# A two-block transformer kernel on one core: the expert gates of token tile 0 as split fp32r products, routing over 112 sums, and a new routing order

## The chip, the cores and the metric

The kernel runs on one core of a Trainium2 chip. The metric is the device time of one execution in microseconds (us). TensorE multiplies matrices, VectorE and ScalarE work elementwise, GpSimd (POOL) issues the gather and scatter transfers, SyncE issues the large loads. Each engine runs its own instructions in the order in which they are written and waits where a tile that it needs isn't ready, or a buffer isn't free.

## The reference

Two transformer blocks on 256 tokens of width 1024. The change lies in the last part of the second block, a layer of 16384 experts (`peer_ffn`). For each of 256 tokens and 8 heads:

```python
q = (xn @ w_q).reshape(B, S, 8, 2, 64)
s = einsum('bshpd,hpkd->bshpk', q, sub_keys)          # two score rows of 128 a head
v_half, i_half = top_k(s, 16)                         # the 16 best of each
cand = v_half[..., 0, :, None] + v_half[..., 1, None, :]   # 16 x 16 sums
top_s, top_c = top_k(cand.reshape(..., 256), 16)      # the 16 best sums
i1 = take(i_half[..., 0, :], top_c // 16); i2 = take(i_half[..., 1, :], top_c % 16)
experts = i1 * 128 + i2;  g = softmax(top_s)
u = expert_u[experts]                                 # 128 experts a token
act = gelu(einsum('cd,ced->ce', x, u))
out = einsum('ce,ced->cd', g * act, expert_v[experts])
```

## The kernel before, in words

The kernel doesn't gather experts. It multiplies all tokens with all 16384 rows of `u`, and all weighted activations with all rows of `v`, and a table of gates [expert, token] that is zero nearly everywhere picks what counts.

**U part.** A loop of 128 steps (`for i in range(P)`). Step i multiplies one block of 128 experts (1024 x 128 of `u`) with the 256 tokens. To keep fp32 accuracy with the fast fp32r format, a number is split into a high half (rounded to fp32r) and a low half (the rest), and a product is three fp32r products: `u_mm` issues 24 TensorE matmuls of 256 columns (L1029 to L1031). `u_load` loads the block and makes its high half on ScalarE (L1016), `u_low` makes its low half on VectorE (L1021), both for step i + 2 while step i runs. `u_act` applies the gelu to step i - 1 on ScalarE; steps below 88 send the result to memory from ScalarE's queue (L1041, L1042), later ones keep it (`kept`, L1038). The high halves have three buffers.

**Routing.** VectorE fills what the products leave it. `route` yields small pieces with an estimated cost each: `half` (the 16 best of 128 scores, by MAX8, FIND_INDEX8 and MATCH_REPLACE8), `both` (256 sums and the 16 best of them), `places` and `pick` (back from positions to indices), `share` (softmax). A generator `steps` gives the order: tile 1 (tokens 128 to 255) in four pairs of heads, then tile 0 with its 8 heads together. In step i pieces are issued while the estimated VectorE time `dve` is below TensorE's `pe`.

**Gates of tile 1** go through memory: `share` computes addresses and `scatter` issues 16 indirect transfers a head on GpSimd (L1085), 128 in all; a head's wait for those of the head before. `g_load` reads the table back (L1199), and its first load waits for the last head's scatters.

**Gates of tile 0** are made on chip. `turn` transposes indices and gates (L1099) once tile 0 is routed. Then one group of 4 tokens is made in each step, 32 groups in all: `g_prep` makes two one-hot rows a token on VectorE (two instructions of 512 elements, L1178) and multiplies the second by the gate (L1180); in the next step `g_mm` multiplies the two one-hots of a token, 128 x 128 in fp32, 4 matmuls a group (L1186, each stands twice in the trace), and in the step after that ScalarE copies 4 tokens' gates into the table `gb` (L1187).

**V part.** 128 steps of 12 matmuls of 512 columns (L1293 to L1295), whose weights are activations times gates (`w_mul`, `w_split`).

From the U part on, the order on TensorE, VectorE, ScalarE and SyncE is the order in which the code is written.

Of the kernel before, what the change touches and what calls it, by code (L numbers as in the profile page):

```python
# [10 lines left out]
F32 = mybir.dt.float32  # L11
F32R = mybir.dt.float32r
U32 = mybir.dt.uint32
AF = mybir.ActivationFunctionType
# [5 lines left out]
P = 128  # L20
# [151 lines left out]
def tile_block(ctx, tc, d, out, NK=40, CONV="0.2 0.2 1.1 1.1 1.2", K1=4, M0=7, MR=65, ML=8, MQ=40, WB=3, NTAIL=2, WARM=7):  # L172
# [4 lines left out]
    def nm(s):  # L177
        uid[0] += 1
        return f"{s}_{uid[0]}"
# [813 lines left out]
    with ExitStack() as sc_:  # L993
        pc = Even(sc_.enter_context(tc.tile_pool(name="pc", bufs=1)))
        act_d = dram.tile([P - NK, P, S], F32, name="act_d")
        iT = pc.tile([P, 2, P], F32, name="iT")
        gT = pc.tile([P, P], F32, name="gT")
        gb = pc.tile([P, P, P], F32, name="gb")
        ixr = pc.tile([P, 8, 16], U32, name="ixr")
        gtr = pc.tile([P, 8, 16], F32, name="gtr")  # L1000
# [65 lines left out]
                                                            for e in ("PE", "DVE", "Activation", "SP")}))  # L1066
        i16 = cst[:, C_I16:C_I16 + 16]
        tok = cst[:, C_TOK:C_TOK + 1]
        later = []
        SYNC = mybir.DependencyInfo(mybir.DependencyClass.Sync, mybir.DependencyReason.DATA)  # L1070

        def top16(src, vv, ii, tag, w):
# [22 lines left out]
        def turn(sel):  # L1095

            t = gp()[:, 0:384].rearrange("p (i t) -> p i t", i=3)
            for i in range(3):
                T.transpose(t[:, i, :], sel[:, i].rearrange("p h s -> p (h s)"), ident)  # L1099
            A.activation(iT, t[:, 0:2], AF.Copy)  # L1100
            A.activation(gT, t[:, 2, :], AF.Copy)
            done.append(0)

        def route(tt, heads, sel):

            n = len(heads)
            H = slice(heads[0], heads[0] + n)
            vals = rk.tile([P, 8, 2, 16], F32, name=nm("vals"), tag="vals", bufs=1)
            idx = rk.tile([P, 8, 2, 16], U32, name=nm("idx"), tag="idx", bufs=1)
            tv = rk.tile([P, 8, 16], F32, name=nm("tv"), tag="tv")  # L1110
            ti = rk.tile([P, 8, 16], U32, name=nm("ti"), tag="ti", bufs=1)
            te = rk.tile([P, 8, 16], F32, name=nm("te"), tag="te")
            idf = rk.tile([P, 8, 2, 16], F32, name=nm("idf"), tag="idf", bufs=1)
            ab = rk.tile([P, 2, 8, 16], U32, name=nm("ab"), tag="ab", bufs=1)
            abf = rk.tile([P, 2, 8, 16], F32, name=nm("abf"), tag="abf", bufs=1)

            def half(k, p_):
                top16(sco[:, tt, heads[k], p_, :], vals[:, k, p_, :], idx[:, k, p_, :], "mr", P)

            def both(k):  # L1120
                cand = rk.tile([P, 16, 16], F32, name=nm("cand"), tag="cand")
                V.tensor_tensor(cand, vals[:, k, 0, :, None].to_broadcast([P, 16, 16]),
                                vals[:, k, 1, None, :].to_broadcast([P, 16, 16]), op=OP.add)
                top16(cand.rearrange("p a b -> p (a b)"), tv[:, k, :], ti[:, k, :], "mc", S)

            def places():
                V.tensor_tensor(te[:, :n], tv[:, :n], tv[:, :n, 0:1].to_broadcast([P, n, 16]), op=OP.subtract)
                V.tensor_copy(idf[:, :n], idx[:, :n])
                V.tensor_scalar(ab[:, 0, :n], ti[:, :n], 4, None, op0=OP.logical_shift_right)
                V.tensor_scalar(ab[:, 1, :n], ti[:, :n], 15, None, op0=OP.bitwise_and)  # L1130
                V.tensor_copy(abf[:, :, :n], ab[:, :, :n])
                later.append(lambda: A.activation(te[:, :n], te[:, :n], AF.Exp))

            def pick(p_, k0, m):
                k_ = slice(k0, k0 + m)
                e_ = rk.tile([P, 4, 16, 16], F32, name=nm("eq"), tag="eq")[:, :m]
                V.tensor_tensor(e_, abf[:, p_, k_, :, None].to_broadcast([P, m, 16, 16]),
                                i16[:, None, None, :].to_broadcast([P, m, 16, 16]), op=OP.is_equal)
                V.tensor_tensor(e_, e_, idf[:, k_, p_, None, :].to_broadcast([P, m, 16, 16]), op=OP.mult)
                V.tensor_reduce(sel[:, p_, heads[0] + k0:heads[0] + k0 + m, :], e_, axis=AX.X, op=OP.add)  # L1140

            def share():
                zs = rk.tile([P, 8], F32, name=nm("zs"), tag="zs")
                V.tensor_reduce(zs[:, :n], te[:, :n], axis=AX.X, op=OP.add)
                V.reciprocal(zs[:, :n], zs[:, :n])
                dst = gtr[:, H] if tt else sel[:, 2, H]
                V.tensor_tensor(dst, te[:, :n], zs[:, :n, None].to_broadcast([P, n, 16]), op=OP.mult)
                if tt == 0:
                    later.append(lambda: turn(sel))
                    return  # L1150
                f = rk.tile([P, 8, 16], F32, name=nm("cf"), tag="cf", bufs=1)
                V.scalar_tensor_tensor(f[:, :n], sel[:, 1, H], float(P), tok[:, :, None].to_broadcast([P, n, 16]),
                                       op0=OP.mult, op1=OP.add)
                V.scalar_tensor_tensor(ixr[:, H], sel[:, 0, H], float(P * P), f[:, :n], op0=OP.mult, op1=OP.add)
                for h in heads:
                    scatter(h)

            for k in range(n):
                for p_ in range(2):
                    yield 1.57, lambda k=k, p_=p_: half(k, p_)  # L1160
            for k in range(n):
                yield 2.75, lambda k=k: both(k)
            yield 1.4 if n > 4 else 1.0, places
            for p_ in range(2):
                for k0 in range(0, n, 4):
                    m = min(4, n - k0)
                    yield 0.9 * m, lambda p_=p_, k0=k0, m=m: pick(p_, k0, m)
            yield 1.2, share


        iota = cst[:, C_IOTA:C_IOTA + P]

        def g_prep(t4):

            t_ = slice(4 * t4, 4 * t4 + 4)
            oh = [po_.tile([P, 4, P], F32, name=nm("oh"), tag=f"oh{i}", bufs=2) for i in range(2)]
            for i, o in enumerate(oh):
                V.tensor_tensor(o, iota[:, None, :].to_broadcast([P, 4, P]),  # L1178
                                iT[:, i, t_, None].to_broadcast([P, 4, P]), op=OP.is_equal)
            V.tensor_tensor(oh[1], oh[1], gT[:, t_, None].to_broadcast([P, 4, P]), op=OP.mult)  # L1180
            later.append(lambda: g_mm(t4, oh))

        def g_mm(t4, oh):
            pt = ga_().rearrange("p (t i) -> p t i", t=4)
            for q_ in range(4):
                T.matmul(pt[:, q_, :], oh[0][:, q_, :], oh[1][:, q_, :], start=True, stop=True)  # L1186
            later.append(lambda: A.activation(gb[:, :, 4 * t4:4 * t4 + 4], pt.rearrange("p t i -> p i t"), AF.Copy))  # L1187


        pw = None  # L1190
# [41 lines left out]
        def w_step():  # L1232
            if not ws and wq_:
                w_mul(wq_.pop(0))
            if ws:
                k = next(iter(ws))
                if wq_:
# [5 lines left out]
        done = []  # L1243
        sel1 = pr.tile([P, 2, 8, 16], F32, name="sel1")
        sel0 = pr.tile([P, 3, 8, 16], F32, name="sel0")
        steps = (st_ for tt, heads, sel in ((1, (0, 1), sel1), (1, (2, 3), sel1), (1, (4, 5), sel1), (1, (6, 7), sel1),
                                            (0, tuple(range(8)), sel0)) for st_ in route(tt, heads, sel))
        nxt = next(steps)
        g_left = list(range(P // 4))
        dve, pe = 0.0, 0.0  # L1250
# [1 line left out]
        for i in range(P):  # L1252

            now, later = later, []
            q = p
            p = u_mm(*prep.pop(0))
            if q is not None:
                u_act(i - 1, q)
            for f in now:
                f()  # L1260
            h = u_load(i + 2)
            dve += 1.2
            pe += 2.9

            if g_left and done:
                g_prep(g_left.pop(0))
                dve += 2.0
                pe += 0.88
            while nxt is not None and dve < pe:
                dve += nxt[0]  # L1270
                nxt[1]()
                nxt = next(steps, None)
            if i >= P - 2:
                w_step()
            prep.append(u_low(*h))
            if nxt is None and pw is None and done:
                sr.close()
                pk = Even(sg_.enter_context(tc.tile_pool(name="pk", bufs=1)))
                kept.append(pk.tile([P, NK, S], F32, name="kept"))
                pw = Even(sg_.enter_context(tc.tile_pool(name="pw", bufs=1, side="right")))  # L1280
            if i == P - 12:
                for _ in range(3):
                    a_load()
                    g_load()
        u_act(P - 1, p)
        assert not g_left and not later

        pO = [[op_(), op_()], [gp(), gp()]]

# [82 lines left out]
```

## Time and profile before

| | |
|---|---|
| time, median of 3 runs | 1203.9 us (1203.32 to 1205.07) |
| the profiled execution: its time, its span | 1205.83 us, 1204.0 us |
| TensorE busy | 1165.1 us, 97% |
| VectorE busy | 929.2 us, 77% |
| ScalarE busy | 634.6 us, 53% |
| GpSimd busy | 335.4 us, 28% |
| the U part (first to last matmul of L1029) | 443.3 to 842.8 us |

Busy shares are means over stages with different limits, so the rows further down are taken by stage. [...]

### The profile page before, as it was taken

To read this page: it belongs to the slowest core of one execution; us is meant where nothing else is said; L and a number is where in the kernel's file an instruction comes from. 1 tells how busy PE (TensorE), PEld (TensorE's weight loads), DVE (VectorE), ACT (ScalarE), POOL (GpSimd) and SP (SyncE) were. 2 spreads that over 40 slices of the span, in tenths; PEclk is the share of its full clock that TensorE was granted. 3 is DMA by queue.
4 is the path that set the end of the run, shared out by engine and by line. 5 is a ranking of instruction groups with operands and counts; after the bars stand their busy time and mean duration, and the time that the engine had idled before them with its cause. 6 is when DMAs were issued, how large, how long until landed. Compare 5 with 4: busy or idle time off the path is not lost.

```text
span 1204.0 us, 20173 instructions
## 1 busy us (share of the span) xinstructions
PE 1165.1 (97%) x7282; PEld 1043.8 (87%) x7282; DVE 929.2 (77%) x1907; ACT 634.6 (53%) x1050; POOL 335.4 (28%) x278
## 2 busy tenths in 40 slices
PE   8999999979998899999999999999999999999995
PEld 7777886869997799999999999999888888888884
DVE  5786978976676849999999888854777777777775
ACT  6557554575345555555545555554545555555553
POOL 2001200022012002787778778400111111111102
PEclk9999999989899899999999999999999999999998
DMA  8876689749454557889888886645877777778773
GB/s 288 291 251 247 241 232 349 272 153 378 149 202 149 151 172 233 225 220 238 225 232 211 206 169 142 192 161 182 256 244 248 253 250 249 251 248 256 255 229 134
DMA packets 103315, 271.94 MB, mean 226 GB/s; under 512 B 28637, under 2 KB 40421, under 8 KB 102704
## 3 DMA queue, kind: packets, MB, share of 16 engines
q1 hardware_dynamic: 62352, 225.03, 57.0%
q0 software_dynamic: 27616, 31.87, 12.4%
q10 hardware_dynamic: 13248, 13.77, 3.4%
q8 instruction: 57, 0.93, 0.3%
q14 instruction: 42, 0.34, 0.1%
HBM read 248.51 MB, written 23.68 MB: 226 GB/s over the span
## 4 chain that ended last, share of the span: by engine, by line
PE 83%; DVE 6%; DMA 4%; ACT 2%; issue 2%; POOL 1%; SPq 0%; ACTq 0%; POOLq 0%; DVEq 0%
PE sc L1031 10%; PE sc L1030 10%; PE sc L1029 10%; PE po L1293 5%; PE po L1294 5%; PE po L1295 5%; PE pg L1293 5%; PE pg L1294 5%; PE pg L1295 5%; PE pg L279 4%; PE pg L280 4%; PE pg L278 4%; PE pg L1186 2%; DVE wl L253 2%; DMA wf<-in_w_in_dram 2%
## 5 line engine op out<-in xcount | busy, mean ns | idle before, releaser
L1021 DVE TENSOR_TENSOR wl<-wf,wh 128x1024 fp32r<-128x1024 f32 x256 | 311.9, 1221 | 107.2 <-ACT wh L1016 105.0
L1029 PE MATMUL sc<-hThi,wh 128*128 128x256 f32 x1024 | 292.5, 286 | 0.0
L1031 PE MATMUL sc<-hThi,wl 128*128 128x256 f32 x1024 | 290.5, 284 | 0.8 <-DVE wl L1021 0.5
L1030 PE MATMUL sc<-hTlo,wh 128*128 128x256 f32 x1024 | 289.7, 283 | 0.0
L1016 ACT ACTIVATE wh<-wf 128x1024 fp32r<-128x1024 f32 x256 | 268.9, 1050 | 38.1 <-ACT act L1041 15.3
L1085 POOL DMA_INDIRECT g_d<-gtr,ixr x128 | 231.1, 1806 | 123.8 <-ACT act L1041 64.0
L1031 PEld LDWEIGHTS sc<-hThi,wl 128*128 128x128 f32 x1024 | 196.3, 192 | 2.0 <-DVE wl L1021 1.5
L1029 PEld LDWEIGHTS sc<-hThi,wh 128*128 128x128 f32 x1024 | 196.6, 192 | 0.0
L1030 PEld LDWEIGHTS sc<-hTlo,wh 128*128 128x128 f32 x1024 | 196.4, 192 | 0.0
L253 DVE TENSOR_TENSOR wl<-wf,wh 128x1024 fp32r<-128x1024 f32 (+3 forms) x121 | 138.4, 1151 | 58.8 <-ACT wh L252 58.5
L252 ACT ACTIVATE wh<-wf 128x1024 fp32r<-128x1024 f32 (+3 forms) x121 | 120.2, 996 | 114.2 <-PE pg L280 57.2
L252 ACT ACTIVATE wwh<-w 128x256 fp32r<-128x256 f32 x128 | 53.5, 418 | 167.7 <-PE pg L1294 167.7
L278 PE MATMUL pg<-wh,hThi 128*128 128x512 f32 (+1 forms) x264 | 102.2, 388 | 1.7 <-ACT hThi L345 1.7
L279 PE MATMUL pg<-wl,hThi 128*128 128x512 f32 (+1 forms) x264 | 102.8, 389 | 0.4 <-DVE wl L253 0.4
L280 PE MATMUL pg<-wh,hTlo 128*128 128x512 f32 (+1 forms) x264 | 102.1, 388 | 0.0
L1293 PE MATMUL po<-wh,wwh 128*128 128x512 f32 x256 | 99.6, 389 | 0.0
L1294 PE MATMUL po<-wl,wwh 128*128 128x512 f32 x256 | 99.6, 389 | 0.0
L1295 PE MATMUL po<-wh,wwl 128*128 128x512 f32 x256 | 99.6, 389 | 0.0
L1293 PE MATMUL pg<-wh,wwh 128*128 128x512 f32 x256 | 99.6, 389 | 0.0
L1294 PE MATMUL pg<-wl,wwh 128*128 128x512 f32 x256 | 99.6, 389 | 0.0
L1295 PE MATMUL pg<-wh,wwl 128*128 128x512 f32 x256 | 99.6, 389 | 0.0
L1211 POOL DMA_DIRECT2D actl<-act_d x44 | 31.9, 725 | 189.0 <-DVE w L1219 108.8
(384 smaller groups left out, 2066.5 us busy)
## 6 DMA issues: line engine op xcount, KB each, us to landing
wf<-in_u_dram SPq DMA_DIRECT2D x128, 512.0 KB
wf<-in_v_dram SPq DMA_DIRECT2D x128, 512.0 KB
wf<-in_w_in_dram SPq DMA_DIRECT2D x68, 512.0 KB
wm<-in_w_mod_dram SPq DMA_DIRECT2D x48, 512.0 KB
act_d<-act ACTq DMA_DIRECT2D x88, 128.0 KB
actl<-act_d POOLq DMA_DIRECT2D x44, 256.0 KB
wf<-in_w_out_dram SPq DMA_DIRECT2D x16, 512.0 KB
g_d<-zero POOLq DMA_DIRECT2D x16, 512.0 KB
```

What stands on the lines that cost most here:

```text
L252: A.activation(hi, src, AF.Copy)
L253: (lo_eng or V).tensor_tensor(lo, src, hi.bitcast(F32), op=OP.subtract)
L279: T.matmul(p, lh[:, k, t], l_, start=False, stop=False)
L1016: A.activation(h, f, AF.Copy)
L1021: V.tensor_tensor(l, f, h.bitcast(F32), op=OP.subtract)
L1029: T.matmul(p, h[:, o], hThi[:, k, :], start=(k == 0), stop=False)
L1030: T.matmul(p, h[:, o], hTlo[:, k, :], start=False, stop=False)
L1031: T.matmul(p, l[:, o], hThi[:, k, :], start=False, stop=(k == KD - 1))
L1085: q_ = nc.gpsimd.indirect_dma_start(g_flat, bass.IndirectOffsetOnAxis(ap=ixr[:, h, j:j + 1], axis=0), gtr[:, h, j:j + 1], None, compute_op ...
L1293: T.matmul(pO[tt][n], wh[:, t_], h[:, c_], start=first, stop=False)
L1294: T.matmul(pO[tt][n], wh[:, t_], l[:, c_], start=False, stop=False)
L1295: T.matmul(pO[tt][n], wl[:, t_], h[:, c_], start=False, stop=last)
```

## The change

1. **Gates of tile 0.** The transposed gates are kept as a high half `gTh` (fp32r) and a low half `gTl`. `g_prep` no longer multiplies by the gate; one of its one-hots is fp32r. A new `g_gate`, one step later, makes for each of the 4 tokens the second one-hot times the high and times the low half, side by side in one tile of 256 columns: 8 ScalarE instructions of 128 elements, each with a per-partition scale. `g_mm`, again a step later, does one fp32r product of 256 columns a token, two tokens to a PSUM tile. After that VectorE adds the two halves and writes `gb`, 2 instructions a group, in place of ScalarE's copy. While pieces of routing are left, a group is begun in every third step, then in two of three.
2. **Sums.** Of the 256 sums of a head 112 remain: the first 4 of one row with all 16 of the other, and the other 12 with the first 4. `sums` makes them for up to 4 heads with two instructions, `both` searches 112 in place of 256, and `places` takes three instructions more to turn positions back into pairs.
3. **Order of routing.** Tile 0 is routed before the last pair of heads (6, 7) of tile 1.

```diff
+        later, gates = [], []
+        NC = 4 * 16 + 12 * 4
...
-            A.activation(gT, t[:, 2, :], AF.Copy)
+            A.activation(gTh, t[:, 2, :], AF.Copy)
+            V.tensor_tensor(gTl, t[:, 2, :], gTh.bitcast(F32), op=OP.subtract)
...
+            def sums(k0, m):
+                for a0, na_, nb in ((0, 4, 16), (4, 12, 4)):
+                    V.tensor_tensor(cand[:, k0:k0 + m, 16 * a0:16 * a0 + na_ * nb].rearrange("p k (a b) -> p k a b", b=nb),
+                                    vals[:, k0:k0 + m, 0, a0:a0 + na_, None].to_broadcast([P, m, na_, nb]),
+                                    vals[:, k0:k0 + m, 1, None, 0:nb].to_broadcast([P, m, na_, nb]), op=OP.add)
             def both(k):
-                cand = rk.tile([P, 16, 16], F32, name=nm("cand"), tag="cand")
-                V.tensor_tensor(cand, vals[:, k, 0, :, None].to_broadcast([P, 16, 16]),
-                                vals[:, k, 1, None, :].to_broadcast([P, 16, 16]), op=OP.add)
-                top16(cand.rearrange("p a b -> p (a b)"), tv[:, k, :], ti[:, k, :], "mc", S)
+                top16(cand[:, k, :], tv[:, k, :], ti[:, k, :], "mc", NC)
...
+            for k0 in range(0, n, 4):
+                m = min(4, n - k0)
+                yield 0.2 + 0.12 * m, lambda k0=k0, m=m: sums(k0, m)
             for k in range(n):
-                yield 2.75, lambda k=k: both(k)
-            yield 1.4 if n > 4 else 1.0, places
+                yield 1.6, lambda k=k: both(k)
+            yield 2.2 if n > 4 else 1.6, places
...
-            V.tensor_tensor(oh[1], oh[1], gT[:, t_, None].to_broadcast([P, 4, P]), op=OP.mult)
-            later.append(lambda: g_mm(t4, oh))
-        def g_mm(t4, oh):
-            pt = ga_().rearrange("p (t i) -> p t i", t=4)
+            gates.append(lambda: g_gate(t4, oh))
+        def g_gate(t4, oh):
+            b = po_.tile([P, 4, 2, P], F32R, name=nm("ohg"), tag="ohg", bufs=2)
             for q_ in range(4):
-                T.matmul(pt[:, q_, :], oh[0][:, q_, :], oh[1][:, q_, :], start=True, stop=True)
-            later.append(lambda: A.activation(gb[:, :, 4 * t4:4 * t4 + 4], pt.rearrange("p t i -> p i t"), AF.Copy))
+                for i, g_ in enumerate((gTh.bitcast(F32), gTl)):
+                    A.activation(b[:, q_, i, :], oh[1][:, q_, :], AF.Copy, scale=g_[:, 4 * t4 + q_:4 * t4 + q_ + 1])
+            later.append(lambda: g_mm(t4, oh[0], b))
+        def g_mm(t4, o, b):
+            for q0 in (0, 2):
+                pt = ga_().rearrange("p (t c i) -> p t c i", t=2, c=2)
+                for q_ in range(2):
+                    T.matmul(pt[:, q_].rearrange("p c i -> p (c i)"), o[:, q0 + q_, :],
+                             b[:, q0 + q_].rearrange("p c i -> p (c i)"), start=True, stop=True)
+                later.append(lambda pt=pt, t=4 * t4 + q0: V.tensor_reduce(
+                    gb[:, :, t:t + 2], pt.rearrange("p t c i -> p i t c"), axis=AX.X, op=OP.add))
...
-        steps = (... (1, (0, 1), sel1), (1, (2, 3), sel1), (1, (4, 5), sel1), (1, (6, 7), sel1), (0, tuple(range(8)), sel0) ...
+        steps = (... (1, (0, 1), sel1), (1, (2, 3), sel1), (1, (4, 5), sel1), (0, tuple(range(8)), sel0), (1, (6, 7), sel1) ...
...
-            if g_left and done:
+            now, gates = gates, []
+            for f in now:
+                f()
+            if g_left and done and i % 3 in ((0, 1) if nxt is None else (0,)):
                 g_prep(g_left.pop(0))
-                dve += 2.0
-                pe += 0.88
+                dve += 2.9
+                pe += 0.5
```

On TensorE, at a step of the U part with a group of gates, the rows before are these (`sc` is the sum of a step, `wh` and `wl` are the halves of its block, `hThi` and `hTlo` those of the tokens, `pg` holds gates, `oh` are one-hots; the last 3 of the 24 matmuls of one step, then the first of the next):

```order
L1030 MATMUL sc_8313<-hTlo,wh_8261 128x256
L1031 MATMUL sc_8313<-hThi,wl_8268 128x256
L1186 MATMUL pg_8340<-oh_8307,oh_8306 128x128 x4
L1029 MATMUL sc_8356<-hThi,wh_8304 128x256
L1030 MATMUL sc_8356<-hTlo,wh_8304 128x256
```

And in the changed kernel (`ohg` are one-hots times gate halves):

```order
L1031 MATMUL sc_8080<-hTlo,wh_8023 128x256
L1032 MATMUL sc_8080<-hThi,wl_8029 128x256
L1210 MATMUL pg_8108<-ohg_8065,oh_8025 128x256 x2
L1210 MATMUL pg_8111<-ohg_8065,oh_8025 128x256 x2
L1030 MATMUL sc_8129<-hThi,wh_8063 128x256
```

Four fp32 products of 128 columns have become four fp32r products of 256, at the same place between two steps.

On ScalarE, in one step after step 88 and the start of the next, before (`kept` is the gelu of a step, `wh` the high half of a block, `gb` the gate table):

```order
L1038 ACTIVATE kept<-sc_8313 128x256
L1187 ACTIVATE gb<-pg_8340 128x128x4
L1016 ACTIVATE wh_8390<-wf_8388 128x1024
L1038 ACTIVATE kept<-sc_8356 128x256
L1187 ACTIVATE gb<-pg_8383 128x128x4
```

And in the changed kernel, from the last gate instructions of one step to the first of the next:

```order
L1203 ACTIVATE ohg_8209<-oh_8170,gTh 128x128
L1203 ACTIVATE ohg_8209<-oh_8170,gTl 128x128
L1039 ACTIVATE kept<-sc_8175 128x256
L1017 ACTIVATE wh_8258<-wf_8256 128x1024
L1203 ACTIVATE ohg_8260<-oh_8219,gTh 128x128
L1203 ACTIVATE ohg_8260<-oh_8219,gTl 128x128
```

The copy to `gb` has left ScalarE, and 8 short scaled instructions (here the last two of one step and the first two of the next) stand behind the high half in each such step, ahead of the next gelu. On VectorE the changed kernel has, in such a step, two reductions into `gb`, two one-hots and the low half, where before it had two one-hots, the multiplication and the low half. The scatters and loads of GpSimd and the loads of SyncE stand in the same order as before. In the changed kernel tile 0 is routed by the end of step 61 and the pair (6, 7) in step 79 (its last instruction stands in front of the low half of block 81); 6 groups of gates are begun before that, in every third step from 63 on, and 26 after, in two of three steps from 81 to 118.

## Rows read from the trace of the kernel before

**Rows 1.** Windows: stretch, busy us of PE, PEld, DVE, ACT, POOL; clock, DMA.

```profile
443.00:676.00 233.00, 232.16 (x1923) 230.96 (x1922) 212.61 (x547) 128.11 (x175) 159.64 (x86) 1.00 0.84 222
676.00:800.00 124.00, 124.00 (x1055) 124.00 (x1055) 101.91 (x130) 64.40 (x101) 75.45 (x49) 1.00 0.68 167
800.00:843.10 43.10, 43.10 (x361) 43.10 (x361) 19.74 (x24) 20.62 (x32) 0.00 (x0) 1.00 0.55 181
```

**Rows 2.** Page, part 4: shares of the chain that ended last, by engine.

```profile
PE 83%; DVE 6%; DMA 4%; ACT 2%; issue 2%; POOL 1%; SPq 0%; ACTq 0%; POOLq 0%; DVEq 0%
```

**Rows 3.** Line L1029: kinds, count, duration ns, first and last start us.

```profile
L1029 PE MATMUL sc<-hThi,wh x1024: 277/283/469, 443.3 to 842.8; 128*128 128x256 f32 x171
```

**Rows 4.** Chain in order of time, 640 to 680 and 830 to 860 us: start, length, what.

```profile
646.71 1.28 ACT L1132
...
676.33 0.33 PE pg L1099 x3
...
843.32 0.23 PE po L1293
```

**Rows 5.** ScalarE timeline: start, length, instruction [idle before it and its releaser].

```profile
475.38 0.38 ACT L1041 ACTIVATE act<-sc 128x256 f32<-128x256 f32 x1 [0.98 <-PE sc L1031]
478.26 0.38 ACT L1041 ACTIVATE act<-sc 128x256 f32<-128x256 f32 x1 [0.98 <-PE sc L1031]
...
677.13 1.06 ACT L1016 ACTIVATE wh<-wf 128x1024 fp32r<-128x1024 f32 x1
678.08 0.39 ACT L1041 ACTIVATE act<-sc 128x256 f32<-128x256 f32 x1
678.92 1.06 ACT L1016 ACTIVATE wh<-wf 128x1024 fp32r<-128x1024 f32 x1 [0.46 <-ACT act L1041]
...
690.92 0.39 ACT L1041 ACTIVATE act<-sc 128x256 f32<-128x256 f32 x1 [1.33 <-PE sc L1031]
694.69 0.38 ACT L1041 ACTIVATE act<-sc 128x256 f32<-128x256 f32 x1 [1.33 <-PE sc L1031]
```

**Rows 6.** Groups by line and form: TensorE and VectorE: count | busy us, mean ns | idle.

```profile
L1186 PE MATMUL pg<-oh,oh 128*128 128x128 f32 x256 | 33.7, 275 | 0.0
L1140 DVE TENSOR_REDUCE sel<-eq 128x32 f32<-128x512 f32 x8 | 5.5, 687 | 0.3
L1341 DVE TENSOR_TENSOR wf<-wf,tmf 128x512 f32<-128x512 f32 x4 | 3.4, 842 | 0.1
L1077 DVE MAX8 tv<-mc 128x8 f32<-128x256 f32 x16 | 6.9, 428 | 0.6
L1077 DVE MAX8 vals<-mr 128x8 f32<-128x128 f32 x32 | 9.4, 295 | 1.1
```

**Rows 7.** VectorE timeline at two gate tiles.

```profile
677.11 1.30 DVE L1178 TENSOR_TENSOR oh<-cst,iT 128x512 f32<-128x512 f32 x2 [3.51 <-issue]
678.51 0.69 DVE L1180 TENSOR_TENSOR oh<-oh,gT 128x512 f32<-128x512 f32 x1
679.12 1.22 DVE L1021 TENSOR_TENSOR wl<-wf,wh 128x1024 fp32r<-128x1024 f32 x1
680.26 1.29 DVE L1178 TENSOR_TENSOR oh<-cst,iT 128x512 f32<-128x512 f32 x2
```

**Rows 8.** Groups by line and form, ScalarE; the same columns.

```profile
L369 ACT ACTIVATE hf<-sc,modc 128x128 f32<-128x128 f32 x16 | 6.0, 458 | 2.3 <-DVE cbias L824 2.3
L501 ACT ACTIVATE pm<-pm,mn 128x128 f32<-128x128 f32 x16 | 6.3, 392 | 4.9 <-DVE mn L497 4.9
...
L1101 ACT ACTIVATE gT<-pg 128x128 f32<-128x128 f32 x1 | 0.3, 273 | 0.0
```

**Rows 9.** ScalarE timeline, a run of eight scaled instructions.

```profile
264.29 2.88 ACT L369 ACTIVATE hf<-sc,modc 128x128 f32<-128x128 f32 x8
```

**Rows 10.** GpSimd timeline: scatters of tile 1, then the first gate load.

```profile
701.12 1.67 POOL L1085 DMA_INDIRECT g_d<-gtr,ixr  x1 [2.81 <-DVE oh L1178]
...
767.18 0.61 POOL L1199 DMA_DIRECT2D gl<-g_d  x1 [2.17 <-DMA g_d<-gtr,ixr]
```

More of the change, by code (lines that the diff above doesn't have):

```diff
@@ L996, in tile_block @@
         iT = pc.tile([P, 2, P], F32, name="iT")
-        gT = pc.tile([P, P], F32, name="gT")
+        gTh = pc.tile([P, P], F32R, name="gTh")
+        gTl = pc.tile([P, P], F32, name="gTl")
         gb = pc.tile([P, P, P], F32, name="gb")
@@ L1068, in tile_block @@
         tok = cst[:, C_TOK:C_TOK + 1]
-        later = []
+        later, gates = [], []
+        NC = 4 * 16 + 12 * 4
         SYNC = mybir.DependencyInfo(mybir.DependencyClass.Sync, mybir.DependencyReason.DATA)
@@ L1115, in route @@
             abf = rk.tile([P, 2, 8, 16], F32, name=nm("abf"), tag="abf", bufs=1)
+            cand = rk.tile([P, 8, NC], F32, name=nm("cand"), tag="cand", bufs=1)
             def half(k, p_):
                 top16(sco[:, tt, heads[k], p_, :], vals[:, k, p_, :], idx[:, k, p_, :], "mr", P)
+            def sums(k0, m):
[3 more added lines that the diff above has]
+                                    vals[:, k0:k0 + m, 1, None, 0:nb].to_broadcast([P, m, na_, nb]), op=OP.add)
             def both(k):
-                cand = rk.tile([P, 16, 16], F32, name=nm("cand"), tag="cand")
-                V.tensor_tensor(cand, vals[:, k, 0, :, None].to_broadcast([P, 16, 16]),
-                                vals[:, k, 1, None, :].to_broadcast([P, 16, 16]), op=OP.add)
-                top16(cand.rearrange("p a b -> p (a b)"), tv[:, k, :], ti[:, k, :], "mc", S)
+                top16(cand[:, k, :], tv[:, k, :], ti[:, k, :], "mc", NC)
             def places():
@@ L1129, in places @@
                 V.tensor_scalar(ab[:, 0, :n], ti[:, :n], 4, None, op0=OP.logical_shift_right)
-                V.tensor_scalar(ab[:, 1, :n], ti[:, :n], 15, None, op0=OP.bitwise_and)
-                V.tensor_copy(abf[:, :, :n], ab[:, :, :n])
+                V.tensor_scalar(ab[:, 1, :n], ti[:, :n], 2, None, op0=OP.logical_shift_right)
+                V.scalar_tensor_tensor(abf[:, 0, :n], ab[:, 1, :n], -12.0, ab[:, 0, :n], op0=OP.add, op1=OP.max)
+                V.tensor_scalar(abf[:, 1, :n], abf[:, 0, :n], 4.0, 48.0, op0=OP.mult, op1=OP.add)
+                V.scalar_tensor_tensor(abf[:, 1, :n], abf[:, 0, :n], 16.0, abf[:, 1, :n], op0=OP.mult, op1=OP.min)
+                V.tensor_tensor(abf[:, 1, :n], ti[:, :n], abf[:, 1, :n], op=OP.subtract)
                 later.append(lambda: A.activation(te[:, :n], te[:, :n], AF.Exp))
@@ L1175, in g_prep @@
             t_ = slice(4 * t4, 4 * t4 + 4)
-            oh = [po_.tile([P, 4, P], F32, name=nm("oh"), tag=f"oh{i}", bufs=2) for i in range(2)]
+            oh = [po_.tile([P, 4, P], F32R if i == 0 else F32, name=nm("oh"), tag=f"oh{i}", bufs=2) for i in range(2)]
             for i, o in enumerate(oh):
@@ L1245, in tile_block @@
         sel0 = pr.tile([P, 3, 8, 16], F32, name="sel0")
-        steps = (st_ for tt, heads, sel in ((1, (0, 1), sel1), (1, (2, 3), sel1), (1, (4, 5), sel1), (1, (6, 7), sel1),
-                                            (0, tuple(range(8)), sel0)) for st_ in route(tt, heads, sel))
+        steps = (st_ for tt, heads, sel in ((1, (0, 1), sel1), (1, (2, 3), sel1), (1, (4, 5), sel1),
+                                            (0, tuple(range(8)), sel0), (1, (6, 7), sel1)) for st_ in route(tt, heads, sel))
         nxt = next(steps)
@@ L1285, in tile_block @@
         u_act(P - 1, p)
-        assert not g_left and not later
+        assert not g_left and not later and not gates
         pO = [[op_(), op_()], [gp(), gp()]]
```

## The prediction, made before the changed kernel was run

> **What bounds the kernel now.** First I read the chain of waits by engine: 83% of it is TensorE [rows 2]. Then the windows by stage: in the U part, where the whole change lies, TensorE is busy in 232.2 of 233.0, 124.0 of 124.0 and 43.1 of 43.1 us at the full granted clock of 1.00 [rows 1]. The reader is to see that VectorE comes near it in the first stretch (212.6 of 233.0), less in the second (101.9 of 124.0), and that ScalarE has the most room (128.1 and 64.4). So the U part lasts as long as TensorE's instructions, provided that the other two deliver in time.
>
> The U part can be added up. The gelu of a step starts when its matmuls end, so the distance of two of them is the length of a step: 478.26 - 475.38 = 2.88 us without gates, which is 0.12 us for each of 24 fp32r matmuls of 256 columns, and 694.69 - 690.92 = 3.77 us with a group of gates [rows 5]. A group thus costs TensorE 0.89 us. 128 x 2.88 = 368.6, 32 x 0.89 = 28.5, the transposes 0.3 [rows 4]: 397.4 us. From the first matmul at 443.3 [rows 3] to the V part's first at 843.3 [rows 4] there are 400.0. The missing 2.6 us are waits; the chain leaves TensorE for them around 646.7, where ScalarE loads a table for the exponentials of eight heads [rows 4].
>
> **The change, part by part.**
>
> *Gate products.* The 256 rows of L1186 [rows 6] are 32 groups of 4 fp32 products. In their place a group has 4 fp32r matmuls of 256 columns, the very shape that goes at 0.12 us: 0.48 us. Nothing hides a TensorE instruction here, so 32 x (0.89 - 0.48) = 13.1 us go from the path. This is the main term. Its bounds: the new product can't be quicker than 0.12 us, and if waits come with it they belong to the terms below.
>
> *Gate halves on ScalarE.* 32 x 8 = 256 instructions of 128 elements from SBUF with a per-partition scale come in; 32 copies go. No row shows this one. With two per-partition operands 128 elements from PSUM take 458 ns, with none 273, so one operand is about 93; from SBUF with one they take 392 [rows 8]. I take 0.39 us. But length isn't rate: eight of the 458 ns ones in a row last 2.88 us, so one starts (2.88 - 0.46) / 7 = 0.35 us after another, 0.11 less than its length [rows 9]. With that overlap the new ones come every 0.28 us. Bounds: 0.16 us (273 ns with overlap) and 0.46 us (the dearer one without). I take 0.28, since a large instruction from SBUF overlaps as much: a high half of 1.06 us lets the gelu start after 0.95 [rows 5].
>
> In the crowded stretch, steps 81 to 121 with 26 groups in 13 threes of steps, TensorE needs 3 x 2.88 + 2 x 0.48 = 9.6 us for three steps. ScalarE needs 3 x (0.95 for a high half + 0.27 for the gelu, with 0.08 of slack: 1.3) + 16 x 0.28 = 8.4 us. It fits. Before step 88, where the gelu's result is also sent from its queue, gelu and issue take 678.92 - 678.08 = 0.84 us [rows 5], and three steps come to 5.4 + 4.5 = 9.9 us; that is 0.3 us over, for two threes. High halves are made two steps ahead, which leaves a lead of about 3 us (two steps of 2.88 to 3.36 us, less a gelu, a high and a low half), so nothing is lost there. What is queued behind a group's 8 instructions is the next gelu and the next high half; they come up to 2.3 us later, inside the lead.
>
> *VectorE.* A gate step before is two one-hots at 1.40 us (677.11 to 678.51), a multiplication at 0.61 and a low half at 1.14 [rows 7]. The multiplication goes; two reductions come, from 512 elements in PSUM to 256. The nearest row is the reduction of 512 at 687 ns, the dearest VectorE row of 512 shown is 842 [rows 6]; less the same overlap of 0.08 that is 0.61 to 0.76. I take 0.61. Three steps with two groups: 2 x (1.40 + 1.22 + 1.14) + 1.14 = 8.7 us of 9.6; at the upper bound 9.3, which still fits. A reduction waits for the products issued in the step before and has the one-hots and a low half behind it; that low half isn't needed for another step and a half.
>
> *112 sums.* A search takes 428 ns over 256 and 295 over 128 [rows 6], so about 280 over 112. Five searches and a sum a head are some 1.0 us less, 16 us over 16 heads; `places` gives back about 0.6 us in each of five calls. VectorE is not on the path, so I cost this at nothing. It does bring the end of routing forward, which is where the room for the spread-out gates comes from.
>
> *Order of routing.* The pair (6, 7) is ready in step 79, at about 443.3 + 80 x 2.88 + 5 x 0.48 + 2.9 = 679 us. Before, the scatters of its first head began at 701.1, behind those of earlier heads [rows 10]. So GpSimd's row of scatters isn't moved, and its first gate load stays near 767.2 [rows 10], while the U part ends near 830. Cost nothing; the cover is 63 us.
>
> *Turning tile 0.* In step 62 VectorE's subtraction for `gTl` waits for the transposes and the two copies, and a routing piece of some 1.6 us and the low half of block 64 are queued behind it. By the old trace the copies end some 0.9 us after the transposes begin; 0.9 + 0.25 + 1.6 + 1.2 = 4.0 us against 0.33 + 2.88 + 0.24 = 3.45 when TensorE wants that half. I charge 0.6 us, once (0 to 1).
>
> The 2.6 us of old waits I leave as they are: the table loads remain, VectorE's load around them is lighter by little. They may go (2.6 to the good) or double.
>
> Sum: 13.1 - 0.6 = 12.5 us. The profiled execution would go from 1205.8 to 1193.3 us (span 1204.0 to 1191.5); from the median of 1203.9, 1.9 us under the profiled one, I get 1191.4 us.
>
> **The rivals.**
>
> *ScalarE's short instructions don't overlap.* In rows 9 the eight read PSUM, the new ones read SBUF. At 0.39 us each three steps take 3.9 + 6.2 = 10.1 us against 9.6; 0.5 x 13 = 7 us less the lead of 3: 4 us given back, 1195.4 us. Against it stands the overlap behind the high half [rows 5]. [...]
>
> *ScalarE becomes the bound outright: slower.* At 0.46 us each (no overlap, and the price of two operands) three steps take 3.9 + 7.3 = 11.2 us; 1.6 x 13 = 21 less 3 is 18 us lost in steps 81 to 121 against 12.5 won: 1209 us. It decides from 0.43 us on, since (3.9 + 16 x 0.43 - 9.6) x 13 - 3 = 12. For it: the row of 458 ns. Against it: one operand, not two, and rows 9.
>
> *The reductions cost double.* Their innermost run has 2 elements, where the rows have 16. At 1.22 us long three steps take 2 x (1.40 + 2.28 + 1.14) + 1.14 = 10.8 us on VectorE; 1.2 x 13 - 3 = 12.6 us given back: 1204, no change. Against it: the reduction's rows go by their input alone.
>
> *More than forecast.* If the lighter VectorE takes the old waits away as well, 12.5 + 2.6 gives 1188.8 us.
>
> **How the numbers follow.** TensorE stays the bound: 0.80, with a range of its own of 1188.8 to 1194. Short instructions without overlap, or another give-back of that size: 0.09 (1194 to 1201). Reductions or a new wait that eat it all: 0.05. Slower by ScalarE or otherwise: 0.06. About 0.2%, 2.4 us, is what a measurement tells from no change; so faster 0.88, same 0.06, slower 0.06. The range of 8 in 10 is 1188.3 to 1196.5.
>
> **What would show it.** Right: the U part from 443 to about 830 us; gelus 2.88 us apart without gates and 3.36 with; TensorE's gate rows 0.12 us apart; ScalarE's new rows near 0.39 us long and 0.28 apart; reductions near 0.69 us; GpSimd's first gate load near 767. Wrong: gelu distances over 3.4 us in steps 81 to 121, with TensorE idle behind a low half or a gate half of ScalarE; or a first gate load later than the end of the U part.

## The result, and the profile after

The changed kernel takes 1191.7 us (median of 5 runs, 1190.99 to 1194.35) against 1203.94 us before (1203.32 to 1205.07): ratio 0.9903, 95% interval 0.989 to 0.9916. Forecast were 1191.4 us. The profiled execution took 1190.99 us, its span is 1189.2 us.

The windows of the U part (columns as in [rows 1]) in the changed kernel:

```profile
439.40:676.00 236.60, 234.92 (x1946) 233.63 (x1945) 212.76 (x575) 139.24 (x218) 167.96 (x86) 1.00 0.84 218
676.00:800.00 124.00, 123.57 (x1026) 122.96 (x1025) 107.30 (x145) 109.29 (x281) 79.77 (x49) 1.00 0.76 190
800.00:828.40 28.40, 28.40 (x239) 28.40 (x238) 17.27 (x24) 16.65 (x35) 0.00 (x0) 1.00 0.57 182
```

TensorE is still busy nearly throughout, at a granted clock of 1.00. What the reader is to see is the second stretch: there ScalarE has gone from 64.4 us [rows 1] to 109.3 of 124, and VectorE from 101.9 to 107.3.

The first matmul of the U part (the row that answers to [rows 3]):

```profile
L1030 PE MATMUL sc<-hThi,wh x1024: 277/283/469, 439.4 to 827.9; 128*128 128x256 f32 x171
```

And the chain of waits in order of time, around the table load of tile 0, its turning, and a late group of gates with the store behind it, then the first matmul of the V part (answers to [rows 4]):

```profile
591.63 0.31 ACT te L1145
...
622.62 0.34 PE pg L1101 x3
...
623.57 0.29 DVE gTl L1104
...
625.36 1.22 DVE wl L1022
...
646.72 2.44 ACT ohg L1203 x8
649.16 0.27 ACT act L1042
649.45 5.25 DMA act_d<-act
654.78 0.39 ACT act L1042
...
828.47 0.23 PE po L1323
```

So the U part goes from 439.4 to 828.5: 389.1 us against 400.0, 10.9 less. The rest of the difference of the two spans (14.8 us) lies ahead of the U part, which begins 3.9 us earlier although its instructions stand in the same order. Some 3 us of that goes with TensorE's clock in a stretch near 310 us: from the first matmul of L830 to that of L854 there are 8.6 us before and 5.6 in the changed kernel. Before (columns as in [rows 1]; the third from the end is the granted clock):

```profile
310.00:312.00 2.00, 2.00 (x11) 2.00 (x11) 1.35 (x5) 1.10 (x2) 0.00 (x0) 0.50 0.01 4
```

The same place in the changed kernel:

```profile
308.70:310.70 2.00, 2.00 (x19) 2.00 (x18) 1.88 (x5) 1.48 (x2) 0.00 (x0) 1.00 0.01 4
```

With 0.50 of the clock granted the 2 us hold 11 matmuls, with 1.00 they hold 19. The stretch comes and goes between executions of the same kernel, as a later run shows (0.50 in e9, below), and is no part of the change. This is why the U part of a trace is the better measure here, and why the medians, 12.2 us apart, are nearer to it than the two spans. A U part is not exact either: two traces of the changed kernel have 389.1 and 388.6 us (e9 below).

ScalarE's timeline in three steps (start, length, instruction), answering to [rows 5, 9]:

```profile
744.35 0.36 ACT L1039 ACTIVATE kept<-sc 128x256 f32<-128x256 f32 x1
744.61 1.05 ACT L1017 ACTIVATE wh<-wf 128x1024 fp32r<-128x1024 f32 x1
745.56 0.39 ACT L1203 ACTIVATE ohg<-oh,gTh 128x128 fp32r<-128x128 f32 x1
745.85 0.39 ACT L1203 ACTIVATE ohg<-oh,gTl 128x128 fp32r<-128x128 f32 x1
...
747.90 0.36 ACT L1039 ACTIVATE kept<-sc 128x256 f32<-128x256 f32 x1
...
750.36 0.38 ACT L1039 ACTIVATE kept<-sc 128x256 f32<-128x256 f32 x1 [1.14 <-PE sc L1032]
...
753.93 0.36 ACT L1039 ACTIVATE kept<-sc 128x256 f32<-128x256 f32 x1
...
757.48 0.37 ACT L1039 ACTIVATE kept<-sc 128x256 f32<-128x256 f32 x1
```

The new scaled instructions come 745.85 - 745.56 = 0.29 us apart. The gelus at 747.90, 750.36, 753.93 and 757.48 are 2.46, 3.57 and 3.55 us apart, since those behind gate instructions start late. Together they give three steps of 9.58 us, which is 3 x 2.88 + 2 x 0.47: a group of gates costs TensorE 0.47 us where it cost 0.89. The idle 1.14 us ahead of the gelu at 750.36 is all that ScalarE has to spare in three steps.

The groups by line and form that answer to [rows 6, 8]:

```profile
L1203 ACT ACTIVATE ohg<-oh,gTh 128x128 fp32r<-128x128 f32 x128 | 50.1, 391 | 0.0
L1212 DVE TENSOR_REDUCE gb<-pg 128x256 f32<-128x512 f32 x64 | 41.1, 683 | 3.1 <-PE pg L1210 3.0
L1075 DVE MAX8 tv<-cand 128x8 f32<-128x112 f32 x16 | 4.3, 271 | 0.1
```

GpSimd's scatters of head 6 and the first gate load, answering to [rows 10]:

```profile
700.10 1.55 POOL L1087 DMA_INDIRECT g_d<-gtr,ixr  x1 [3.18 <-DMA g_d<-gtr,ixr]
...
771.66 0.62 POOL L1225 DMA_DIRECT2D gl<-g_d  x1 [1.11 <-DMA g_d<-gtr,ixr]
```

The scatters of head 6 begin where they began. Counted from the start of the U part they are 2.9 us later and the load 8.4, which still leaves it 57 us ahead of the V part.

### The profile page after: what moved, and what is told of

It reads as the page before. It is cut to its first block, busy times and chain, and to the rows that moved or that the text cites. A ratio compares the mean times of both kernels' runs of the same rounds, so it can differ in the third digit from the quotient of the medians.

```text
span 1189.2 us, 20240 instructions
## 1 busy us (share of the span) xinstructions
PE 1150.3 (97%) x7154; PEld 1028.3 (86%) x7154; DVE 932.3 (78%) x1951; ACT 686.8 (58%) x1274; POOL 348.0 (29%) x278
## 4 chain that ended last, share of the span: by engine, by line
PE 78%; DVE 7%; DMA 5%; ACT 5%; issue 3%; POOL 1%; ACTq 0%; SPq 0%; POOLq 0%; DVEq 0%
PE sc L1032 9%; PE sc L1031 9%; PE sc L1030 9%; PE po L1325 5%; PE po L1324 5%; PE po L1323 5%; PE pg L1325 5%; PE pg L1324 5%; PE pg L1323 5%; PE pg L279 4%; PE pg L280 4%; PE pg L278 4%; DVE wl L253 2%; DMA wf<-in_w_in_dram 2%; ACT ohg L1203 2%
## 5 line engine op out<-in xcount | busy, mean ns | idle before, releaser
L1087 POOL DMA_INDIRECT g_d<-gtr,ixr x128 | 243.8, 1904 | 121.1 <-ACT act L1042 61.7
```

Source lines behind the costliest of these rows:

```text
L1087: q_ = nc.gpsimd.indirect_dma_start(g_flat, bass.IndirectOffsetOnAxis(ap=ixr[:, h, j:j + 1], axis=0), gtr[:, h, j:j + 1], None, compute_op ...
```

## The experiments

Times are compared with the kernel before on the same chip. The U part is taken from each trace, from its first matmul to the first of the V part.

| kernel | time us | ratio (95% interval) | U part us |
|---|---|---|---|
| before | 1203.9 | | 400.0 |
| changed | 1191.7 | 0.9903 (0.9890 to 0.9916) | 389.1 |
| e1 old product | 1202.8 | 0.9996 (0.9984 to 1.0009) | 400.3 |
| e2 product alone | 1190.7 | 0.9890 (0.9874 to 0.9907) | 387.8 |
| e3 order back | 1191.8 | 0.9898 (0.9880 to 0.9915) | 387.6 |
| e4 a group every step | 1197.7 | 0.9963 (0.9951 to 0.9975) | 394.1 |
| e5 10 gate rows | 1194.9 | 0.9917 (0.9900 to 0.9934) | 393.0 |
| e6 12 gate rows | 1213.0 | 1.0076 (1.0060 to 1.0093) | 408.6 |
| e7 halves added in PSUM | 1202.4 | 0.9990 (0.9980 to 1.0001) | 399.9 |
| e8 high half only | 1188.9 | 0.9880 (0.9864 to 0.9897) | 385.5 |
| e9 changed, again | 1193.3 | 0.9907 (0.9884 to 0.9929) | 388.6 |
| e10 three store buffers | 1189.2 | 0.9872 (0.9855 to 0.9890) | 386.9 |
| e11 order back, three buffers | 1189.9 | 0.9882 (0.9866 to 0.9899) | 387.6 |

**e1, the old product under the new routing.**

```diff
-    b[:, q_, i, :] <- oh[1] * (gTh, gTl) on ScalarE; T.matmul(pt, o, b)   # 256 columns, fp32r
+    V.tensor_tensor(oh[1], oh[1], gT..., op=OP.mult)
+    T.matmul(pt[:, q_, :], oh[0][:, q_, :], oh[1][:, q_, :])              # 128 columns, fp32
-    dve += 2.9; pe += 0.5
+    dve += 2.0; pe += 0.88
```

> The changed kernel with the old gate product alone put back (fp32, 128 columns, one-hot multiplied on VectorE, copy on ScalarE); the 112 sums and the new routing order stay. Theory A, the gain is the TensorE time of the gate product: 32 x 0.41 us come back, 1202 to 1205 us, U part about 400 us long. Rival B, a good part of the gain comes from lighter and reordered routing: 1195 to 1199 us, U part below 396 us.

Measured: 1202.8 us and a U part of 400.3. The whole gain is gone: the lighter sums and the new order are worth nothing that can be measured by themselves (the interval of the ratio is 0.9984 to 1.0009).

**e2, the product alone.**

```diff
-    top16(cand[:, k, :], tv[:, k, :], ti[:, k, :], "mc", NC)          # 112 sums
+    top16(cand.rearrange("p a b -> p (a b)"), tv[:, k, :], ti[:, k, :], "mc", S)   # 256 sums
-    steps: (1, (4, 5)), (0, all), (1, (6, 7))
+    steps: (1, (4, 5)), (1, (6, 7)), (0, all)
-    i % 3 in ((0, 1) if nxt is None else (0,))
+    (i % 4 != 3 if nxt is None else i % 3 == 0)
```

> The split fp32r product alone: 256 sums and the old routing order are put back, and, since routing then ends later, a group of gates is begun in three of four steps so that all 32 fit. Theory A: sums and order only make room; ScalarE needs 4 x 1.21 + 24 x 0.293 = 11.9 us and VectorE 4 x 1.13 + 3 x 2.4 = 11.7 us for four steps of 13.0 on TensorE, so the gain stays: 1190 to 1193.5 us. Rival B, sums and order carry part of it: 1196 us or more.

Measured: 1190.7 us, U part 387.8, as much as with all three parts. So the product is the change; the other two parts only set where the groups stand, and a rule of three steps in four does as well.

**e3, the old order alone.**

```diff
-    steps: (1, (4, 5)), (0, all), (1, (6, 7))
+    steps: (1, (4, 5)), (1, (6, 7)), (0, all)
```

> The changed kernel with tile 0 routed last again. Theory A: the pair (6, 7) waits for GpSimd's earlier scatters either way and 32 groups in two of three steps fit behind step 73: 1190.5 to 1193 us, scatters ending within 3 us of the changed kernel's. Rival B, the order matters (gates crowded at the end of the U part make TensorE wait): 1194.5 us or more.

Measured: 1191.8 us, in theory A's range. The U part is even 1.5 us shorter than the changed kernel's (1.0 shorter than in e9, the changed kernel once more). Theory A's other sign failed: the scatters end at 781.4 us where the changed kernel's end at 769.7, not within 3 us. That costs nothing, because the first gate load, at 785.0, is still 45 us ahead of the V part.

**e4, a group of gates in every step.**

```diff
-    i % 3 in ((0, 1) if nxt is None else (0,))
+    (nxt is None or i % 3 == 0)
```

> The changed kernel with a group of gates begun in every step once routing is done, in place of two of three. A step then takes 3.36 us on TensorE, 0.95 + 0.26 + 8 x 0.293 = 3.56 on ScalarE and 2.40 + 1.13 = 3.53 on VectorE. Theory A: ScalarE is the bound by 0.2 us a step, 26 x 0.2 = 5 us less the lead of about 3 us: 1193 to 1195 us, gelus about 3.56 us apart at the end of the row of groups. Rival B, the lead hides all of it: 1191 to 1192.5. Rival C, waits between the engines come on top: over 1196.

Measured: 1197.7 us, the U part 394.1, 5.0 more. ScalarE's timeline (three gelus with groups in every step):

```profile
715.03 0.36 ACT L1039 ACTIVATE kept<-sc 128x256 f32<-128x256 f32 x1
...
718.58 0.36 ACT L1039 ACTIVATE kept<-sc 128x256 f32<-128x256 f32 x1
...
722.14 0.36 ACT L1039 ACTIVATE kept<-sc 128x256 f32<-128x256 f32 x1
```

They are 3.56 us apart, to the hundredth what the instructions add up to, so ScalarE is the bound there. The time lies in rival C's range, but not for rival C's reason. The expectation left out that in the 8 steps before step 88, where the gelu's result is also sent from its queue, a step takes 4.07 us on ScalarE, where TensorE wants 3.36. 8 x 0.71 + 18 x 0.20 = 9.3 us. In TensorE's timeline 5 of the 8 steps and all 18 show such a wait, 7.2 us; the lead takes the first three of the 8, 2.1 us. The U part is only 5.0 us longer because the changed kernel has 2.3 us of waits of its own near 663 to 702 us (see e10), of which e4's trace shows 0.3. So no wait between engines on top is needed to explain the time.

**e5 and e6, more rows on ScalarE.** Two, and four, more instructions of the same kind in each group, whose result nobody reads.

```diff
+    x_ = po_.tile([P, 2 or 3, P], F32R, tag="ohx", bufs=1)
+    for q_ in range(2 or 4):
+        A.activation(x_[:, q_ % 3, :], oh[1][:, q_, :], AF.Copy, scale=gTl[...])
```

> The changed kernel with 2 more ScalarE instructions of the gate kind in each group (128 elements, scaled, written to a tile that nobody reads). Theory A: ScalarE has 1.1 us of 9.6 to spare in three steps with two groups, and 4 x 0.293 = 1.2 us fill it: 1191.5 to 1194 us. Rival, ScalarE is already the bound in the changed kernel: 13 x 1.2 us on top of every three steps, 1204 us or more.

> The changed kernel with 4 more ScalarE instructions of the gate kind in each group. Theory A: from step 88 on three steps take 3 x 1.21 + 24 x 0.293 = 10.7 us on ScalarE against 9.6, before it 12.5; 11 x 1.1 + 2 x 2.9 = 17.6 us less a lead of about 3.5 us, so 14 us lost: 1203 to 1208 us, all of the gain. Rival, waits are hidden by the lead again and again: below 1199 us.

Measured: 1194.9 and 1213.0 us. ScalarE in e6, three steps with two groups:

```profile
743.86 0.40 ACT L1039 ACTIVATE kept<-sc 128x256 f32<-128x256 f32 x1
...
748.59 0.41 ACT L1039 ACTIVATE kept<-sc 128x256 f32<-128x256 f32 x1
...
753.32 0.41 ACT L1039 ACTIVATE kept<-sc 128x256 f32<-128x256 f32 x1
...
754.53 0.42 ACT L1039 ACTIVATE kept<-sc 128x256 f32<-128x256 f32 x1
```

748.59 - 743.86 = 4.73, 753.32 - 748.59 = 4.73, 754.53 - 753.32 = 1.21: 10.7 us in all, as worked out, where TensorE wants 9.6. So ScalarE decides from the point that the row arithmetic gives. Both times came out above their ranges, by 1 and 5 us. In both the steps before 88 were undercounted, those from 63 on with a group in every third step too: counted from the start of the U part, step 88 begins 2.9 us later in e5 and 6.0 us later in e6 than in the changed kernel. After it e5 loses 1.1 us more, although its three steps then take 9.5 us and fit, and e6 loses 13.5. That no lead of 3.5 us shows in e6 is the other part of the miss.

**e7, the halves added in PSUM.**

```diff
-    T.matmul(pt[:, q_] (256 wide), o[:, q0 + q_, :], b[:, q0 + q_] (256 wide), start=True, stop=True)
-    V.tensor_reduce(gb[:, :, t:t + 2], pt..., axis=AX.X, op=OP.add)      # twice a group
+    for c in range(2):
+        T.matmul(pt[:, q_, :], o[:, q_, :], b[:, q_, c, :], start=(c == 0), stop=(c == 1))
+    V.tensor_copy(gb[:, :, 4 * t4:4 * t4 + 4], pt...)
```

> The changed kernel with two fp32r matmuls of 128 columns a token, high and low half added in PSUM, in place of one of 256 columns; VectorE then copies 512 elements once a group instead of reducing 512 twice. It measures the step of an fp32r matmul of 128 columns, which no row shows. If it goes by columns (0.06 us): TensorE's time is unchanged, 1190 to 1193 us. If every matmul takes 0.12 us whatever its width: 32 x 0.48 = 15.4 us on top, 1205 to 1209 us, and putting the halves side by side is what makes the gain.

Measured: 1202.4 us, between the two expectations and near the second. The group in TensorE's timeline, and the two matmuls after it:

```profile
745.42 1.00 PE L1210 MATMUL pg<-ohg,oh 128*128 128x128 f32 x8
746.26 0.33 PE L1030 MATMUL sc<-hThi,wh 128*128 128x256 f32 x1
746.43 0.28 PE L1031 MATMUL sc<-hTlo,wh 128*128 128x256 f32 x1
```

The first matmul behind these rows takes 746.43 - 746.26 = 0.17 us to the next start, not the usual 0.12. So a group is read here from its first row to the second matmul behind it, less 0.12: eight fp32r matmuls of 128 columns cost 746.43 - 745.42 - 0.12 = 0.89 us, 0.11 each. In the changed kernel four of 256 columns:

```profile
746.80 0.64 PE L1210 MATMUL pg<-ohg,oh 128*128 128x256 f32 x4
747.28 0.28 PE L1030 MATMUL sc<-hThi,wh 128*128 128x256 f32 x1
747.40 0.28 PE L1031 MATMUL sc<-hTlo,wh 128*128 128x256 f32 x1
```

0.48 us, 0.12 each. And before, the four fp32 products, which stand as 8 rows:

```profile
683.19 1.05 PE L1186 MATMUL pg<-oh,oh 128*128 128x128 f32 x8
684.00 0.36 PE L1029 MATMUL sc<-hThi,wh 128*128 128x256 f32 x1
684.20 0.28 PE L1030 MATMUL sc<-hTlo,wh 128*128 128x256 f32 x1
```

0.89 us, 0.11 a row, the same as in e7. So 32 x 0.41 = 13.1 us come back, and the U part is only 10.8 us longer because the changed kernel's late waits (2.3 us, see e10) aren't in e7's trace. Half the columns save less than a tenth of a matmul's time (0.11 us for 0.12). In these traces a gate group costs by its number of TensorE rows (0.89 us for 8 in either format, 0.48 for 4), and hardly by the format or the width. Each row has a weight load of its own before and in the changed kernel (256 load rows of L1186 and 128 of L1210 for 32 groups). What sets the 0.11 us, the loading of weights or something else, was not tried.

**e8, the high halves only.**

```diff
-    for i, g_ in enumerate((gTh, gTl)): A.activation(b[:, q_, i, :], ...)
+    A.activation(b[:, q_, :], oh[1][:, q_, :], AF.Copy, scale=gTh...)
-    T.matmul(256 columns);  V.tensor_reduce x2
+    T.matmul(128 columns);  V.tensor_copy
```

> Leaves out the low halves of tile 0's gates: 4 fp32r matmuls of 128 columns a group, 4 ScalarE instructions, one VectorE copy of 512. It halves the columns of the changed kernel's product and keeps the number of matmuls. If TensorE's time goes by the number of matmuls (0.105 us each at 128 columns, as the accumulating variant showed): a group takes 0.42 instead of 0.48 us, 32 x 0.06 = 2 us, and about 1 us of waits on ScalarE's gate rows goes: 1188 to 1191.5 us. If it goes by columns (0.06 us each): 0.24 us a group, 8 us less: 1183 to 1185 us.

Measured: 1188.9 us, U part 385.5. Four matmuls of 128 columns in its timeline:

```profile
745.12 0.56 PE L1208 MATMUL pg<-ohg,oh 128*128 128x128 f32 x4
745.52 0.33 PE L1030 MATMUL sc<-hThi,wh 128*128 128x256 f32 x1
745.69 0.28 PE L1031 MATMUL sc<-hTlo,wh 128*128 128x256 f32 x1
```

745.69 - 745.12 - 0.12 = 0.45 us, 0.11 each. (The 0.105 in the expectation was read to the first matmul behind the group, which is a little short.) Halving the columns saves 0.03 us a group, 1 us in all. The rest of the 3.6 us is waits: 385.5 - 368.6 - 0.3 - 32 x 0.45 = 2.2 us are left for them. So the time lies in the first range, with less of it from the columns and more from the waits than expected, and with e7 it shows that the price goes by the rows.

**e9, the changed kernel once more** (no edit).

> The changed kernel once more, on the same chip as the variant beside it, for a direct comparison and to see whether the short stretch at half clock near 310 us, which the profile of before has and that of the changed kernel has not, comes and goes between runs: 1190 to 1194.5 us.

Measured: 1193.3 us (1188.69 to 1193.66), U part 388.6. Its windows have the stretch at a granted clock of 0.50:

```profile
310.00:312.00 2.00, 2.00 (x11) 2.00 (x10) 1.65 (x3) 0.67 (x2) 0.00 (x0) 0.50 0.02 4
```

The same kernel's first trace had not. From the first matmul of L830 to that of L854 there are 8.6 us here, as before. So the 3 us near 310 us belong to the execution and not to the change; of the 13 traces 7 have such a stretch, longer or shorter.

**e10 and e11, a third buffer for the results that are sent to memory**, in the changed kernel and in that with the old order.

```diff
-    a_ = pc.tile([P, S], F32, name=nm("act"), tag="act", bufs=2)
+    a_ = pc.tile([P, S], F32, name=nm("act"), tag="act", bufs=3)
```

> The changed kernel with three buffers in place of two for the gelu results that are sent to memory. In the changed kernel's trace a gelu waits for the store two steps before in 3 places between 630 and 690 us (5.3 us), behind late gates. If those waits make TensorE's later waits near 663, 666 and 685 us (1.3 us): U part 387.5 to 388.2 us instead of 389.1, and no wait of a gelu for a store in that stretch. If the table load and the gates themselves make them: U part unchanged within 0.3 us.

> The variant with the old routing order and the three buffers together, the best the experiments point to. The old order had a U part of 387.6 us; with the stores' waits gone 386.8 to 387.6 us, and a time of 1189.5 to 1191.5 us, not to be told from the changed kernel by the time alone.

Measured: 1189.2 us with a U part of 386.9, and 1189.9 with 387.6. What ScalarE's gelus waited for from 600 to 700 us (us, times), first in the changed kernel:

```profile
  PE sc L1032: 10.0, 10
  DMA act_d<-act: 5.3, 3
```

and with three buffers:

```profile
  PE sc L1032: 11.3, 10
  issue: 3.0, 3
```

The waits for stores are gone, and the U part is 2.2 us shorter than in the changed kernel's trace, a little more than expected, and 1.7 shorter than in e9's. TensorE's waits at five places from 663 to 702 us, 2.3 us in the changed kernel's trace, are down to one of 0.3. Two of the five:

```profile
667.01 0.39 PE L1032 MATMUL sc<-hThi,wl 128*128 128x256 f32 x1 [0.41 <-DVE wl L1022]
692.56 0.39 PE L1210 MATMUL pg<-ohg,oh 128*128 128x256 f32 x1 [0.19 <-ACT ohg L1203]
```

Not all of that is shown to be the third buffer's. Up to step 80 e4 is the same program as the changed kernel, with two buffers, and its gelus wait for stores there as long (4.5 us in 3 places up to 676 us). Yet TensorE hardly stands. The windows (columns as in [rows 1]) of the changed kernel, then of e4:

```profile
655.00:676.00 21.00, 20.45 (x169) 20.05 (x168) 17.98 (x30) 16.02 (x33) 15.70 (x10) 1.00 0.80 198
655.00:676.00 21.00, 20.97 (x175) 20.77 (x174) 18.63 (x33) 17.79 (x37) 15.52 (x9) 1.00 0.81 210
```

Step 80 begins 236.6 us after the start of the U part in the changed kernel, 236.7 in e9, 235.7 in e4 and 235.8 in e10. So about 0.8 of the 2.2 us comes and goes between executions with two buffers. The rest, 1.3 us (0.8 against e9), falls into steps 80 to 88; it agrees with the store as its cause, but rests on one trace. The third buffer was not tried in the kernel before, whose gelus also wait for stores (3.3 us in 2 places from 600 to 710 us).

In the old order, where gates begin in step 72 with no routing beside them, the gelus wait for a store in one place only (1.7 us in e3's trace), and the third buffer brings nothing (U part 387.6 with either). That a store's wait costs TensorE time only where it meets late gates, routing pieces and a table load, as near 661 us in the changed kernel, fits these traces and was not tried by itself. e10 has the lowest median of the kernels that compute everything, but its interval (0.9855 to 0.9890) touches that of the changed kernel's first comparison and overlaps that of e9, so what the third buffer adds to the time is not told from noise.

## Why the prediction was right, point by point

The mechanism held, and the time (1191.4 forecast, 1191.7 measured) lies in the range; that the two agree so closely is luck. By the U parts the gain is 10.9 us (11.4 with e9's trace), not 12.5, because the waits grew. The medians are 12.2 us apart in the first comparison and 10.0 in e9's, where three executions took 1193.0 to 1193.7 us at a mean granted clock of 0.986 or 0.987 and one 1188.7 at 0.990. These four differ by up to 5.0 us, more than the term that was missed, and the shortest has the highest clock.

*Gate products.* Forecast 32 x 0.41 = 13.1 us; by the steps 32 x (0.89 - 0.47) = 13.4, and by e1 and e2 this part alone carries the gain. The size was right: the row for 256 columns gave the new price, and its lower bound of 0.12 us held (0.47 / 4). What the prediction didn't ask is why the old product was dear: not the fp32r format makes the difference but that 8 rows became 4 (e7).

*Waits.* This is the term that was mis-sized. The U part was to keep its 2.6 us of waits and get 0.6 for the turning. Measured are 389.1 - 368.6 - 0.3 - 32 x 0.47 = 5.2 us (4.7 in e9's trace). TensorE's timeline has 1.6 of them up to 617 us: the old waits fell, and with the new order the one at tile 0's table load went from 648.7 to 598.1 us. (Before, they stood near 521, 547, 649, 658 and 664 us, not only at the table load.) The turning came as worked out: VectorE's subtraction at 623.57, the routing piece, the low half at 625.36 in the chain above; TensorE stood 0.7 us, 0.9 with its after-effects.

A further 2.3 us, from 663 to 702 us, were not forecast. ScalarE's late gelus in steps 63 to 88 found both buffers of their results still being stored (the chain goes through such a store at 649.45 for 5.25 us), and the low half (667.01 above) and the gate halves (692.56) came too late. The prediction asked what is queued behind the gate instructions and named the gelu and the high half, but not the store that a late gelu starts late, and whose buffer the gelu after next needs. It also saw ScalarE 0.3 us over in the threes of steps before step 88 and took the lead to cover it. e10 agrees that the store is part of it, but e4 shows that the same waits for stores can leave TensorE nearly undisturbed up to step 80; how much is the store's stays open.

*ScalarE.* Forecast 0.39 us long and 0.28 apart; measured 0.391 and 0.29. The rival of short instructions that don't overlap is thereby false: at 128 elements from SBUF, too, each starts 0.10 us before the one ahead of it has ended. That ScalarE could be the bound was right as a mechanism: e4 and e6 reach it (3.56 us a step where TensorE wants 3.36, and 10.7 for three where it wants 9.6). Gelus more than 3.4 us apart, with TensorE idle behind a gate half, were to be a sign of being wrong. From step 88 on they are up to 3.57 us apart and TensorE is not idle; before it the sign came true, in the two places near 692 and 702 us, for 0.9 us. (The chances 0.80 and 0.09 add up to 0.89 for faster, where the prediction has 0.88.)

*VectorE.* The reduction took 683 ns for the 687 taken, the search over 112 271 for 280; no cost, as forecast. The rival of a double price for reductions is false. (What was held against it, that reductions go by their input, rested on rows that all add up runs of 16: in the trace of before 512 elements took 687 ns and 1024 took 1220. The new ones, with runs of 2, took the 683.)

*Order.* GpSimd's scatters were hardly moved (700.1 for 701.1), and the new place of the pair (6, 7) costs nothing. But it put six groups among the routing of that pair, its table loads and the stores: e3, with the gates behind all routing, has a U part shorter by 1.0 to 1.5 us, too little to be told by the time.

*What lies outside the U part.* It was taken as unchanged. From the V part's first matmul to the end both traces take 360.7 us; ahead of the U part they differ by 3.9, of which some 3 are the clock's.

## What to carry to other kernels

Where one engine is busy from end to end, count its rows: the change was worth the TensorE rows that it took out times the start-to-start time of a row (in each of 32 groups 8 of 0.11 us became 4 of 0.12), less the waits that came with it. Fewer and wider matmuls made the gain; the same number of rows in fp32r (e7, 0.89 us a group) gave nothing. The work moved to ScalarE made TensorE wait for nothing from step 88 on, where three steps left ScalarE 1.14 us idle, and for 0.20 us a step where a group in every step was too much for it (e4). So sum the engine's instructions over one period of the pattern, in every stretch that differs (here the steps that also store), and follow late instructions to the transfers that they start and the buffers that those hold. Compare stages within traces when the spans differ by more than the stage that was changed.

## What the runs showed of the hardware that was not expected

- From start to start an fp32r matmul with 128 x 128 weights took 0.11 us at 128 columns (e7, e8) and 0.12 at 256 (the changed kernel); one row of an fp32 product of 128 columns took 0.11 (before), and such a product stands as two rows. The windows around them have a granted clock of 1.00 in before, the changed kernel and e8; no window shows it for e7, but its matmuls of 256 columns beside the group start 0.12 us apart as well.
- TensorE's granted clock falls to 0.50 for a few microseconds near 310 us in 7 of the 13 traces and not in the other 6, in executions of the same kernel too (e9 has it, the changed kernel's first trace has not). Where it lasts longest, as before and in e9, it costs about 3 us (8.6 us in place of 5.6 from the first matmul of L830 to that of L854). The U part has 1.00 throughout in the six traces whose windows show it (before, the changed kernel, e3, e8, e10, e11).
